# A four-mixer decoder layer on one core: key mixer, query and value mixers and latent attention rewritten, and the schedule made with other operation times

## The chip, the core and the metric

The kernel runs on one NeuronCore of a Trainium2 chip. Its engines work side by side, each through a queue of its own in order: TensorE (PE in the profile; its weight loads are PEld), VectorE (DVE), ScalarE (ACT), GpSimd (POOL) and SyncE (SP), which here only issues transfers. The metric is the device time of one execution in microseconds (us), the median of several runs.

## The reference

One layer on x of 512 positions and 1024 channels, float32:

```python
h = rms_norm(x, norm1_g)
proj = h @ w_in                       # columns shared by four mixers and the gates
o_a = gated_deltanet(...)             # 4 heads of 128; conv + silu, decay, delta rule
o_b = latent_attention(...)           # 4 heads, 128 plain + 64 rotary dimensions, qk-norm
o_c = spatial_gating(...)             # u * (W_s v + b), W_s lower triangular 128x128
o_d = forgetting_attention(...)       # softmax logits + cumulative log forget gate
projected = einsum("bsiw,iwd->bsid", [o_a, o_b, o_c, o_d], w_branch)
x = x + (sum(sigmoid(gates) * projected)) @ w_out
x = x + square(relu(rms_norm(x) @ w_ff1)) @ w_ff2
```

Inside gated_deltanet, k is normalised per head, `lower = strict(k_beta k^T * decay)` is formed per chunk, and `(I + lower)^-1` is applied to the values and to the decayed keys; q enters through `q k^T * decay`. In latent_attention a logit is the dot product of 128 plain and of 64 rotated dimensions.

## The kernel before, in words

All large products keep float32 accuracy through three matmuls: each operand is split into a high part hi (rounded by ScalarE, L85) and a low part lo (the difference, by VectorE, L86), and `mm3` (L163 to L166) adds hi.hi, hi.lo and lo.hi. Weights come in units of 128x1024: the transfer into `raw` (L116, three buffers, issued by SP), the split into whi and wlo (L85, L86, three buffers), and 24 matmuls of 512 columns. `wunit` (L155) hands out one unit; before that it calls `tick`, which moves every open generator in `gens` on to its next `yield`. All side work (the mixers, the attentions) is written as such generators, so a `yield` means: let one more unit of matmuls go first.

That order of the text is not the final one. The framework's scheduler puts the instructions of each engine in an order: by its own operation times it asks which instructions are ready, and takes of these the one that stands first in the text. The queues are then fixed, with semaphores where an engine must wait for another. Tiles of one tag share the number of buffers in `BUFS` (L35).

The order of the stages: normalisation of x and a first small product (to L415); four key heads, `conv(4 + h)` (L617: ScalarE's product, three VectorE multiply-adds L623, tanh L614, VectorE's product L615 into knT); four units for the spatial gate's u; four for its v; four query heads, four value heads, four for z (L837 to L847); then the gate and branch projections (`branch`, L916) with the scan, latent attention and forgetting attention beside them; the output projection; and the up and down projections with a Strassen-like scheme (L208 to L282).

What the change touches:
- `kmix` (L654), one generator per key head: transposes knT (L657), sums its squares on ScalarE (L660), copies it to kn (L662), loads the head's cumulative decay to all partitions (gb, L668), forms exp(min(gb - gcc, 0)) in UA (VectorE L673, ScalarE L675), times br (GpSimd L676), a masked copy dm (GpSimd L684), then UA = (k k^T) * eb (L686) and the scaled keys KG and KD (GpSimd L688, L689).
- `inverse` (L720): copies the 32x32 diagonal blocks of UA through DRAM (scr, L723) into UB (L725), inverts them in a recurrence of 31 steps on VectorE (L732, L733), and goes on to 128x128 with matmuls.
- `colsum` (L635) and `qmix` (L823): ScalarE's square of a query head into sq (L637), then eight matmuls with a column of ones (L640). `vmix` (L829): transposes a value head. `sgmix` (L796): the spatial gate, at its end the split into oC.
- `mla_rope` (L1105), `mla_tr` (L1115): transposes of q, k, kr and qo; q and k are copied out of PSUM by ScalarE (L1117, L1121), kr and qo by VectorE (L1125). Two heads share one tile qrT, 64 rows each.
- `mla_mm` (L1128): per head and query block one matmul of 128 rows (L1131), one of the head's 64 rows (L1132) and the mask (L1133), each float32 one as two instructions in the trace. `fox_mm` (L1199, matmul at L1200) is its counterpart in forgetting attention, with 128 rows alone.

Of the kernel before, what the change touches and what calls it, by code (L numbers as in the profile page):

```python
# [31 lines left out]
    0, 1536, 2048, 2504, 3016, 3528, 5064, 5068)  # L32
AHEAD, AHEAD_RAW = 2, 3
ROWS = (20, 12, 7, 3)
BUFS = dict(ab=4, A=4, K=4, Q=4, G=4, V=4, R=4, U=4, S=8, cv=4, tr=6)  # L35


@with_exitstack
def trunk(ctx, tc, x, positions, norm1_g, w_in, dn_conv_w, dn_a_log, dn_dt_bias, dn_out_norm_g,
# [18 lines left out]
    def tsl(t):  # L58
        return slice(t * P, (t + 1) * P)
# [21 lines left out]
    def mbank():  # L81
        return psm.tile([P, 512], F32, tag="m", name="m")
# [549 lines left out]
        A.activation(out=s_, in_=src, func=AF.Square)  # L632
        V.tensor_reduce(out=dst, in_=t3(s_), axis=AX.X, op=ALU.add)

    def colsum(src):  # L635
        s_ = W("sq")
        A.activation(out=s_, in_=src, func=AF.Square)  # L637
        pb = mbank()
        for t in range(NT):
            T.matmul(out=pb[:, t:t + 1], lhsT=s_[:, tsl(t)], rhs=one, start=True, stop=True)  # L640
        return pb[:, :NT]

    ssk = small([H, NT], "ssk")
    cm5p = small([16], "cm5p")
    ssq = small([H, NT], "ssq")
# [8 lines left out]
    def kmix(h, kT):  # L654
        yield
        KNT[h] = kT
        pk = tpose(cols(kT))  # L657
        sq = W("sq")
        for t in range(NT):
            A.activation(out=sq[:, tsl(t)], in_=pk[:, tsl(t)], func=AF.Square, accum_out=ssk[:, h, t:t + 1])  # L660
        kn = W("kn")
        A.activation(out=kn, in_=pk, func=AF.Copy)  # L662
        V.tensor_scalar(out=ssk[:, h, :], in0=ssk[:, h, :], scalar1=4 * EPS, scalar2=None, op0=ALU.add)
        rk2 = small([NT], "rk2", bufs=2)
        V.reciprocal(out=rk2, in_=ssk[:, h, :])
        yield
        gb = EGB[h] = W("egb", "Q")
        SY.dma_start(out=gb, in_=cumd[h].partition_broadcast(P))  # L668
        br = small([NT], "br", bufs=2)
        V.tensor_tensor(out=br, in0=rk2, in1=beta[:, :, h], op=ALU.mult)  # L670
        eb = UA[:, hsl[h], :]
        for t in range(NT):
            V.tensor_scalar(out=eb[:, t, :], in0=gb[:, tsl(t)], scalar1=gcc[:, t, h:h + 1], scalar2=0.0,  # L673
                            op0=ALU.subtract, op1=ALU.min)
        A.activation(out=eb, in_=eb, func=AF.Exp)  # L675
        G.tensor_tensor(out=eb, in0=eb, in1=last(br, P), op=ALU.mult)  # L676
        glv = t3(gb)[:, :, P - 1]
        V.tensor_tensor(out=ekd[:, h, :], in0=glv, in1=gcc[:, :, h], op=ALU.subtract)
        A.activation(out=ekd[:, h, :], in_=ekd[:, h, :], func=AF.Exp)
        V.scalar_tensor_tensor(out=ekd[:, h, :], in0=ekd[:, h, :], scalar=-1.0, in1=br, op0=ALU.mult, op1=ALU.mult)  # L680
        A.activation(out=egl[:, h, :], in_=glv, func=AF.Exp)
        A.activation(out=gb, in_=gb, func=AF.Exp)
        dm = DM[h] = W("dm", "A")
        G.tensor_tensor(out=t3(dm), in0=eb, in1=mid(maskI, NT), op=ALU.mult)  # L684
        yield
        V.tensor_tensor(out=eb, in0=t3(mm4(kT, kT)), in1=eb, op=ALU.mult)  # L686
        KG[h], KD[h] = W("kg", "G"), W("kd", "K")
        G.tensor_tensor(out=t3(KG[h]), in0=t3(kn), in1=last(eg[:, :, h], P), op=ALU.mult)  # L688
        G.tensor_tensor(out=t3(KD[h]), in0=t3(kn), in1=last(ekd[:, h, :], P), op=ALU.mult)  # L689

    flat = "p t f -> p (t f)"
    DS = [(D0[:, hsl[h], :].rearrange(flat), DT0[:, hsl[h], :].rearrange(flat)) for h in range(H)]
# [25 lines left out]
                                in1=py[r_, :8 * s].rearrange("p (m f) -> p m f", f=s), op=ALU.subtract)  # L718

    def inverse():  # L720
        for b in range(4):
            bs = slice(32 * b, 32 * b + 32)
            SY.dma_start(out=scr[:, b].rearrange("h j i -> j h i"), in_=UA[bs, :, bs])  # L723
        for q in range(2):
            SY.dma_start(out=UB[64 * q:64 * q + 64], in_=scr.rearrange("h b j i -> (h b) j i"))  # L725
        V.memset(UB.rearrange("p j i -> p (j i)")[:, 0:1024:33], -1.0)
# [69 lines left out]
    def sgmix():  # L796
        for t in range(NT):
            sumsq(rsg[:, t, :], vs[t])
        rsqrt(rsg, rsg, 16, 1.0 / P, EPS, shape=4)
        for t in range(NT):  # L800
            G.tensor_tensor(out=t3(vs[t]), in0=t3(vs[t]), in1=last(rsg[:, t, :], P), op=ALU.mult)
        yield
        V.tensor_tensor(out=t3(wsT), in0=t3(tpose(cols(ws))), in1=mid(maskI, 4), op=ALU.mult)
        yield
        yield
        for g in range(4):
            gs = tsl(g)
            pb = mbank()
            for t in range(NT):
                T.matmul(out=pb[:, tsl(t)], lhsT=vs[t][:, gs], rhs=wsT[:, gs], start=True, stop=True)  # L810
            s_ = W("oc_")
            V.scalar_tensor_tensor(out=t3(s_), in0=t3(pb), scalar=par(R_SG + g), in1=mid(bsb[:, gs], NT),
                                   op0=ALU.mult, op1=ALU.add)
            G.tensor_tensor(out=uT[g], in0=s_, in1=uT[g], op=ALU.mult)
            if g % 2 == 1:
                yield
        for g in range(4):
            oC[g] = WR("oc", "S")
            split(oC[g][0], oC[g][1], uT[g])
# [2 lines left out]

    def qmix(h, qT):  # L823
        yield
        V.tensor_copy(out=ssq[:, h, :], in_=colsum(qT))
        G.tensor_tensor(out=EGB[h], in0=EGB[h], in1=qT, op=ALU.mult)
        V.scalar_tensor_tensor(out=AT[h], in0=mm4(KNT[h], qT), scalar=-1.0, in1=AT[h], op0=ALU.mult, op1=ALU.mult)

    def vmix(h, vT):  # L829
        yield  # L830
        VT[h] = W("v", "V")
        V.tensor_tensor(out=t3(VT[h]), in0=t3(tpose(cols(vT))), in1=last(ssk[:, h, :], P), op=ALU.mult)
# [268 lines left out]
        rsqrt(rq_, rq_, 8, 1.0 / 192, EPS, post=192.0 ** -0.5, shape=2)  # L1101

    def mla_rope(c):
        kr, qo = W("kr"), W("qo")
        krv = kr.rearrange("p (t h f) -> p t h f", h=2, f=64)  # L1105
        V.tensor_tensor(out=krv, in0=krr.unsqueeze(2).broadcast_to([P, NT, 2, 64]),
                        in1=last(rkm[:, :, 2 * c:2 * c + 2], 64), op=ALU.mult)
        qov = qo.rearrange("p (t h f) -> p t h f", h=2, f=64)
        tmp = W("tmp")[:, :256].rearrange("p (t h f) -> p t h f", h=2, f=32)
        tb4 = [tabs[0][:, n].unsqueeze(2).broadcast_to([P, NT, 2, 32]) for n in range(4)]  # L1110
        rope(V, qov, qrv[c][:, :, :, 0:32], qrv[c][:, :, :, 32:64], tb4, tmp)
        return kr, qo

    def mla_tr(c, kr, qo):
        for hh in range(2):  # L1115
            qT = W("qT", "V")
            A.activation(out=qT, in_=tpose(hslice(qns[c], hh)), func=AF.Copy)  # L1117
            qTs.append(qT)
        for hh in range(2):
            kT = W("kT", "G")  # L1120
            A.activation(out=kT, in_=tpose(hslice(kns[c], hh)), func=AF.Copy, scale=gqk[:, 0:1])  # L1121
            kTs.append(kT)
        for src, dst in ((kr, krT), (qo, qrT)):
            r_ = W("krT", "R")
            V.tensor_copy(out=r_, in_=tpose(cols(src)))  # L1125
            dst.append(r_)

    def mla_mm(h, i, ps):  # L1128
        ro = slice(64 * (h % 2), 64 * (h % 2) + 64)
        w = (i + 1) * P  # L1130
        T.matmul(out=ps, lhsT=qTs[h][:, tsl(i)], rhs=kTs[h][:, :w], start=True, stop=False)  # L1131
        T.matmul(out=ps, lhsT=qrT[h // 2][ro, tsl(i)], rhs=krT[h // 2][ro, :w], start=False, stop=False)  # L1132
        T.matmul(out=ps[:, i * P:w], lhsT=identb, rhs=mbias, start=False, stop=True)  # L1133

    def mla_post(h, i, ps, pm, e_):
# [215 lines left out]
```

## Time and profile before

| | us |
|---|---|
| median of three runs | 1034.23 |
| lowest and highest | 1033.84, 1034.94 |
| the profiled execution | 1034.64 |
| its span, first to last instruction | 1032.9 |
| TensorE busy in it | 1010.1 |

The granted TensorE clock is 0.994 of full speed over the span. A busy TensorE in this profile is not one at its peak: the ends of matmuls are modelled and overlap the next start, so pitch is read from starts. A wait is listed with the instruction that waited, the one that released it, the total, the number and the longest. A busy time of a window counts all instructions that overlap it.

### The profile page before, as it was taken

What the parts mean: (1) busy time and instruction counts of PE and PEld (TensorE: products, weight loads), DVE (VectorE), ACT (ScalarE), POOL (GpSimd) and SP (SyncE); (2) the same over time, 40 slices, a digit from 0 to 9 for tenths busy, and PEclk for the clock granted to TensorE, in tenths of its full rate; (3) what the DMA queues carried; (4) which work ended last, traced back from release to release, by engine and by line L of the source; (5) the groups of instructions that cost most, each with busy time, mean ns of one, the idle gap of its engine ahead of it and who ended that gap; (6) DMA issues with size and microseconds to landing.
All of it is one profiled execution on the core that took longest, in us unless ns stands there. A gap on an engine that the chain in (4) does not pass through costs nothing.

```text
span 1032.9 us, 12908 instructions
## 1 busy us (share of the span) xinstructions
PE 1010.1 (98%) x4995; PEld 833.9 (81%) x4995; DVE 610.0 (59%) x992; ACT 422.8 (41%) x724; POOL 172.8 (17%) x210
## 2 busy tenths in 40 slices
PE   7989989999999989999999999999999999999998
PEld 6878877888888867778888888888888888888886
DVE  7784899623654754433365443447687598598541
ACT  6463334332433533434444333245453344256420
POOL 2553235100300420015154021100000000000000
PEclk9999989999999999999999999999999999999999
DMA  6334334212223232222422333337135125211421
GB/s 200 103 103 112 102 69 94 72 55 81 62 84 111 62 102 62 82 62 82 123 81 63 98 106 102 96 114 242 38 102 172 36 79 183 62 42 35 129 77 66
DMA packets 127621, 96.69 MB, mean 94 GB/s; under 512 B 15732, under 2 KB 112064, under 8 KB 127560
## 3 DMA queue, kind: packets, MB, share of 16 engines
q1 hardware_dynamic: 127480, 95.85, 31.6%
q8 instruction: 39, 0.64, 0.3%
q14 instruction: 22, 0.18, 0.1%
q10 hardware_dynamic: 80, 0.03, 0.0%
HBM read 92.96 MB, written 2.90 MB: 93 GB/s over the span
## 4 chain that ended last, share of the span: by engine, by line
PE 86%; DVE 8%; DMA 2%; issue 1%; ACT 1%; POOL 1%; SPq 0%; ACTq 0%; DVEq 0%; POOLq 0%
PE g L164 23%; PE g L166 23%; PE g L165 23%; PE m L164 2%; PE m L165 2%; PE m L166 2%; PE m L986 2%; DMA raw<-in_w_in_dram 2%; PE m L196 1%; DVE wlo L86 1%; PE m L205 1%; PE m L1132 1%; DVE cv L623 1%; PE m L976 1%; PE m L1131 1%
## 5 line engine op out<-in xcount | busy, mean ns | idle before, releaser
L86 DVE TENSOR_TENSOR wlo<-raw,whi 128x1024 fp32r<-128x1024 f32 (+2 forms) x136 | 175.4, 1290 | 229.0 <-ACT whi L85 219.6
L85 ACT ACTIVATE whi<-raw 128x1024 fp32r<-128x1024 f32 (+2 forms) x136 | 142.7, 1049 | 319.3 <-PE g L165 155.3
L164 PE MATMUL g<-h,whi 128*128 128x512 f32 x416 | 167.9, 404 | 0.0
L166 PE MATMUL g<-h,wlo 128*128 128x512 f32 x416 | 164.1, 394 | 0.0
L165 PE MATMUL g<-h,whi 128*128 128x512 f32 x416 | 163.5, 393 | 0.0
L164 PE MATMUL g<-xT,whi 128*128 128x512 f32 x256 | 99.7, 389 | 0.0
L166 PE MATMUL g<-xT,wlo 128*128 128x512 f32 x256 | 99.6, 389 | 0.0
L165 PE MATMUL g<-xT,whi 128*128 128x512 f32 x256 | 99.6, 389 | 0.0
L166 PEld LDWEIGHTS g<-h,wlo 128*128 128x128 f32 x416 | 78.9, 190 | 16.7
L164 PEld LDWEIGHTS g<-h,whi 128*128 128x128 f32 x416 | 78.9, 190 | 16.2 <-issue 0.5
L165 PEld LDWEIGHTS g<-h,whi 128*128 128x128 f32 x416 | 78.9, 190 | 16.0 <-issue 0.5
L939 POOL TENSOR_TENSOR mg<-mg,tg 128x512 f32<-128x512 f32 x24 | 35.6, 1487 | 194.2 <-DVE tg L935 193.9
L166 PEld LDWEIGHTS g<-xT,wlo 128*128 128x128 f32 x256 | 48.1, 188 | 10.0
L164 PEld LDWEIGHTS g<-xT,whi 128*128 128x128 f32 x256 | 48.1, 188 | 10.0
L165 PEld LDWEIGHTS g<-xT,whi 128*128 128x128 f32 x256 | 48.1, 188 | 9.9
L164 PE MATMUL g<-whi,h 128*128 128x512 f32 x128 | 50.8, 397 | 0.0
L166 PE MATMUL g<-whi,h 128*128 128x512 f32 x128 | 49.9, 390 | 0.0
L165 PE MATMUL g<-wlo,h 128*128 128x512 f32 x128 | 49.9, 389 | 0.0
L164 PE MATMUL m<-whi,ah 128*128 128x512 f32 x96 | 37.3, 389 | 0.0
L165 PE MATMUL m<-wlo,ah 128*128 128x512 f32 x96 | 37.3, 389 | 0.0
L166 PE MATMUL m<-whi,al 128*128 128x512 f32 x96 | 37.3, 389 | 0.0
L86 DVE TENSOR_TENSOR wlo<-T,whi 128x1024 fp32r<-128x1024 f32 x18 | 22.0, 1220 | 11.5 <-ACT whi L85 11.4
(404 smaller groups left out, 1988.7 us busy)
## 6 DMA issues: line engine op xcount, KB each, us to landing
raw<-in_w_in_dram SPq DMA_DIRECT2D x68, 512.0 KB
raw<-in_w_ff_dram SPq DMA_DIRECT2D x40, 512.0 KB
raw<-in_w_branch_dram SPq DMA_DIRECT2D x16, 512.0 KB
re<-in_w_ff_dram SPq DMA_DIRECT2D x6, 1024.0 KB
ro<-in_w_ff_dram SPq DMA_DIRECT2D x6, 1024.0 KB
raw<-in_w_out_dram SPq DMA_DIRECT2D x8, 512.0 KB
x<-in_x_dram SPq DMA_DIRECT2D x4, 512.0 KB
x<-in_x_dram SPq DMA_DIRECT2D x8, 256.0 KB
```

The costliest lines, as they stand in the source:

```text
L85: A.activation(out=hi, in_=src, func=AF.Copy)
L86: V.tensor_tensor(out=lo, in0=src, in1=hi.bitcast(F32), op=ALU.subtract)
L164: T.matmul(out=ps, lhsT=lh, rhs=rh, start=start, stop=False, skip_group_check=more)
L165: T.matmul(out=ps, lhsT=lh, rhs=rl, start=False, stop=False, skip_group_check=more)
L166: T.matmul(out=ps, lhsT=ll, rhs=rh, start=False, stop=stop, skip_group_check=more)
L196: T.transpose(out=pb[:, tsl(t)], in_=srcs[t], identity=ident)
L205: T.matmul(out=pb[:, tsl(t)], lhsT=lhsT[:, tsl(t)], rhs=rhs[:, tsl(t)], start=True, stop=True)
L623: V.scalar_tensor_tensor(out=y[:, 3 - k:], in0=ps[:, :n], scalar=par(R_CONV + 12 * k + blkno), in1=y[:, 3 - k:], op0=ALU.mult, op1=ALU.add)
L939: G.tensor_tensor(out=merged[m], in0=merged[m], in1=tgs[b], op=ALU.add)
L976: T.transpose(out=pb[:, tsl(t)], in_=pms[n][:, tsl(t)], identity=ident)
L986: T.matmul(out=pv[:, tsl(m)], lhsT=vblk(h, j), rhs=pts[n][:, o_ + j * P:o_ + (j + 1) * P], start=(j == 0), stop=(j == i))
L1131: T.matmul(out=ps, lhsT=qTs[h][:, tsl(i)], rhs=kTs[h][:, :w], start=True, stop=False)
```

## The change

The buffers of three tags grow, and the framework's descriptor scratch in on-chip memory shrinks from 16384 to 1024 bytes a partition. `kmix` forms exp(-relu(gcc - gb)) on ScalarE straight into dm, sends the diagonal blocks of UA head by head, and does the mask and the scaled keys later; `sgmix`, `qmix` and `vmix` get more yields; latent attention's rotary q is kept per head in a 128-row tile whose other half is zero, and ScalarE does all copies out of PSUM; the scheduler takes its operation times from its timeline simulator. The main lines:

```diff
-BUFS = dict(ab=4, A=4, K=4, Q=4, G=4, V=4, R=4, U=4, S=8, cv=4, tr=6)
+BUFS = dict(ab=4, A=4, K=4, Q=4, G=4, V=4, R=6, U=4, S=8, cv=8, tr=8)
@@ kmix
-        kn = W("kn")
-        A.activation(out=kn, in_=pk, func=AF.Copy)
+        KG[h] = W("kg", "G")
+        A.activation(out=KG[h], in_=pk, func=AF.Copy)
-        eb = UA[:, hsl[h], :]
-        for t in range(NT):
-            V.tensor_scalar(out=eb[:, t, :], in0=gb[:, tsl(t)], scalar1=gcc[:, t, h:h + 1], scalar2=0.0,
-                            op0=ALU.subtract, op1=ALU.min)
-        A.activation(out=eb, in_=eb, func=AF.Exp)
-        G.tensor_tensor(out=eb, in0=eb, in1=last(br, P), op=ALU.mult)
+        dm = DM[h] = W("dm", "A")
+        for t in range(NT):
+            A.activation(out=dm[:, tsl(t)], in_=gb[:, tsl(t)], func=AF.Relu, scale=-1.0, bias=gcc[:, t, h:h + 1])
+        A.activation(out=dm, in_=dm, func=AF.Exp, scale=-1.0)
+        G.tensor_tensor(out=t3(dm), in0=t3(dm), in1=last(br, P), op=ALU.mult)
-        dm = DM[h] = W("dm", "A")
-        G.tensor_tensor(out=t3(dm), in0=eb, in1=mid(maskI, NT), op=ALU.mult)
         yield
-        V.tensor_tensor(out=eb, in0=t3(mm4(kT, kT)), in1=eb, op=ALU.mult)
-        KG[h], KD[h] = W("kg", "G"), W("kd", "K")
-        G.tensor_tensor(out=t3(KG[h]), in0=t3(kn), in1=last(eg[:, :, h], P), op=ALU.mult)
-        G.tensor_tensor(out=t3(KD[h]), in0=t3(kn), in1=last(ekd[:, h, :], P), op=ALU.mult)
+        V.tensor_tensor(out=UA[:, hsl[h], :], in0=t3(mm4(kT, kT)), in1=t3(dm), op=ALU.mult)
+        for b in range(4):
+            bs = slice(32 * b, 32 * b + 32)
+            (A if h == H - 1 and b < 2 else SY).dma_start(out=scr[hsl[h], b].rearrange("h j i -> j h i"), in_=UA[bs, hsl[h], bs])
+        for _ in range(H - h):
+            yield
+        G.tensor_tensor(out=t3(dm), in0=t3(dm), in1=mid(maskI, NT), op=ALU.mult)
+        KD[h] = W("kd", "K")
+        G.tensor_tensor(out=t3(KD[h]), in0=t3(KG[h]), in1=last(ekd[:, h, :], P), op=ALU.mult)
+        G.tensor_tensor(out=t3(KG[h]), in0=t3(KG[h]), in1=last(eg[:, :, h], P), op=ALU.mult)
@@ inverse
-        for b in range(4):
-            bs = slice(32 * b, 32 * b + 32)
-            SY.dma_start(out=scr[:, b].rearrange("h j i -> j h i"), in_=UA[bs, :, bs])
@@ sgmix, before the split into oC
+        for _ in range(4):
+            yield
@@ qmix (colsum goes)
-        V.tensor_copy(out=ssq[:, h, :], in_=colsum(qT))
+        s_ = W("sq")
+        A.activation(out=s_, in_=qT, func=AF.Square)
+        yield
+        pb = mbank()
+        for t in range(NT):
+            T.matmul(out=pb[:, t:t + 1], lhsT=s_[:, tsl(t)], rhs=one, start=True, stop=True)
+        V.tensor_copy(out=ssq[:, h, :], in_=pb[:, :NT])
@@ vmix
         yield
+        yield
@@ mla_rope
+        for hh in range(2):
+            qrT.append(W("qrT", "R"))
+            G.memset(qrT[-1][64 - 64 * hh:128 - 64 * hh], 0.0)
@@ mla_tr
+        pb = tpose(cols(qo))
+        for hh in range(2):
+            r_ = qrT[2 * c + hh]
+            own = slice(64 * hh, 64 * hh + 64)
+            A.activation(out=r_[own], in_=pb[own], func=AF.Copy)
+        r_ = W("krT", "R")
+        A.activation(out=r_, in_=tpose(cols(kr)), func=AF.Copy)
+        krT.append(r_)
...
-        for src, dst in ((kr, krT), (qo, qrT)):
-            r_ = W("krT", "R")
-            V.tensor_copy(out=r_, in_=tpose(cols(src)))
-            dst.append(r_)
@@ mla_mm
-        T.matmul(out=ps, lhsT=qrT[h // 2][ro, tsl(i)], rhs=krT[h // 2][ro, :w], start=False, stop=False)
+        T.matmul(out=ps, lhsT=qrT[h][:, tsl(i)], rhs=krT[h // 2][:, :w], start=False, stop=False)
@@ kernel
-    nc = _bacc.Bacc("TRN2", target_bir_lowering=False, num_devices=1)
+    nc = _bacc.Bacc("TRN2", target_bir_lowering=False, num_devices=1, dynamic_dma_scratch_size=1024)
-    with _tile.TileContext(nc) as tc:
+    with _tile.TileContext(nc, schedule_with_timeline_sim=True) as tc:
```

## Rows read from the trace of the kernel before

**Rows 1.** Page, parts 1 and 5: busy us, share, instructions; a group: busy us, mean ns.

```profile
PE 1010.1 (98%) x4995; PEld 833.9 (81%) x4995; DVE 610.0 (59%) x992; ACT 422.8 (41%) x724; POOL 172.8 (17%) x210
...
L164 PE MATMUL g<-xT,whi 128*128 128x512 f32 x256 | 99.7, 389 | 0.0
```

**Rows 2.** Waits of PE: engine line <- releaser: total us, times, longest.

```profile
PE m L196 <- DVE knT L615: 4.0, 2, 2.7
...
PE m L640 <- ACT sq L637: 3.4, 1, 3.4
...
PE m L1132 <- DVE krT L1125: 2.3, 1, 2.3
...
PE m L196 <- DVE cv L615: 1.0, 1, 1.0
...
PE m L976 <- DVE Pm L967: 0.4, 1, 0.4
```

**Rows 3.** Windows: us, busy us of PE, PEld, DVE, ACT, POOL; PEclk; DMA.

```profile
46.00:80.00 34.00, 29.45 (x142) 23.95 (x142) 27.96 (x59) 21.44 (x66) 15.28 (x13) 0.95 0.32 94
...
75.90:79.20 3.30, 3.30 (x9) 2.56 (x8) 0.51 (x3) 3.29 (x12) 1.79 (x3) 0.51 0.03 5
...
80.00:100.00 20.00, 20.00 (x98) 16.83 (x97) 8.71 (x8) 4.64 (x6) 7.90 (x5) 1.00 0.44 104
...
104.00:148.00 44.00, 40.57 (x184) 34.03 (x184) 40.29 (x87) 14.56 (x20) 10.35 (x7) 0.92 0.31 85
...
134.60:140.80 6.20, 6.19 (x23) 5.61 (x24) 6.20 (x12) 0.63 (x1) 1.59 (x2) 0.50 0.25 75
...
740.00:760.00 20.00, 20.00 (x90) 16.57 (x89) 17.49 (x21) 12.24 (x18) 0.00 (x0) 1.00 0.13 34
```

**Rows 4.** Timeline, 65 to 76 us: start, duration, engine, line, operation.

```profile
65.17 1.04 POOL L676 TENSOR_TENSOR UA<-UA,br 128x512 f32<-128x512 f32 x1 [1.09 <-ACT UA L675]
...
65.22 1.00 DVE L680 SCALAR_TENSOR_TENSOR ekd<-ekd,br 128x4 f32<-128x4 f32 x1
...
75.15 0.66 PE L196 MATMUL m<-ident,knT 128*128 128x128 f32 x4 [2.71 <-DVE knT L615]
```

**Rows 5.** Groups by line, all shapes apart: busy us, mean ns.

```profile
L673 DVE TENSOR_SCALAR UA<-egb,gcc 128x128 f32<-128x128 f32 x16 | 5.7, 382 | 1.3 <-DMA egb<-cumd 1.3
...
L660 ACT ACTIVATE sq<-m 128x128 f32<-128x128 f32 x16 | 4.2, 276 | 1.4 <-PE m L196 1.4
```

**Rows 6.** Timeline of SP's queue, 92 to 99 us.

```profile
92.05 2.44 SPq L723 DMA_DIRECT2D scr<-UA  x4
...
98.32 1.16 SPq L725 DMA_DIRECT2D D<-scr  x2
```

**Rows 7.** Timeline, 361 to 371 us, latent attention's first scores.

```profile
361.50 1.28 ACT L1121 ACTIVATE kT<-m,gqk 128x512 f32<-128x512 f32 x2
...
367.64 1.06 ACT L85 ACTIVATE whi<-raw 128x1024 fp32r<-128x1024 f32 x1 [4.87 <-PE g L165]
...
367.79 1.22 DVE L86 TENSOR_TENSOR wlo<-raw,whi 128x1024 fp32r<-128x1024 f32 x1
...
368.92 1.28 DVE L1125 COPY krT<-m 128x512 f32<-128x512 f32 x2
...
370.26 0.48 PE L1132 MATMUL m<-krT 64*128 64x128 f32 x2 [2.26 <-DVE krT L1125]
```

**Rows 8.** Timeline of PE, latent attention's scores of 256 keys.

```profile
443.44 0.60 PE L1131 MATMUL m<-kT,qT 128*128 128x256 f32 x2
443.97 0.70 PE L1132 MATMUL m<-krT 64*128 64x256 f32 x2
444.60 0.23 PE L1133 MATMUL m<-mbias,identb 128*128 128x128 bf16 x1
```

**Rows 9.** Timeline of PE, forgetting attention's scores of 256 keys, twice.

```profile
560.58 1.03 PE L1200 MATMUL m<-kT,qT 128*128 128x256 f32 x4
561.26 0.58 PE L164 MATMUL g<-h,whi 128*128 128x512 f32 x1
```

More of the change, by code (lines that the diff above doesn't have):

```diff
@@ L633, in sumsq @@
         V.tensor_reduce(out=dst, in_=t3(s_), axis=AX.X, op=ALU.add)
[L635 to L638, printed above, removed]
-        for t in range(NT):
-            T.matmul(out=pb[:, t:t + 1], lhsT=s_[:, tsl(t)], rhs=one, start=True, stop=True)
-        return pb[:, :NT]
     ssk = small([H, NT], "ssk")
@@ L1122, in mla_tr @@
             kTs.append(kT)
-        for src, dst in ((kr, krT), (qo, qrT)):
-            r_ = W("krT", "R")
-            V.tensor_copy(out=r_, in_=tpose(cols(src)))
-            dst.append(r_)
     def mla_mm(h, i, ps):
-        ro = slice(64 * (h % 2), 64 * (h % 2) + 64)
         w = (i + 1) * P
         T.matmul(out=ps, lhsT=qTs[h][:, tsl(i)], rhs=kTs[h][:, :w], start=True, stop=False)
-        T.matmul(out=ps, lhsT=qrT[h // 2][ro, tsl(i)], rhs=krT[h // 2][ro, :w], start=False, stop=False)
+        T.matmul(out=ps, lhsT=qrT[h][:, tsl(i)], rhs=krT[h // 2][:, :w], start=False, stop=False)
         T.matmul(out=ps[:, i * P:w], lhsT=identb, rhs=mbias, start=False, stop=True)
```

## The prediction

> **What bounds the kernel now.** The page's first part comes first: TensorE is busy 98% of the span, VectorE 59%, ScalarE 41%, GpSimd 17% [rows 1]. A matmul's bar is longer than its pitch (0.389 us [rows 1] against 90 starts in 20 us, one per 0.22 us [rows 3]), so the share says only that TensorE almost always has work. A change off TensorE can therefore return only what TensorE waits, what it runs at the lower clock, and what a matmul loses between its neighbours. So the second view is TensorE's waits [rows 2]. Leaving out the start and the tail, five entries matter: 4.0 us on knT in two waits, 3.4 us on sq, 2.3 us on krT, 1.0 us on cv, 0.4 us on Pm. The third view is the windows [rows 3]. After two of these waits the granted clock stands at the lower level, 1.2 GHz: 3.30 us at 0.51 behind the 2.71 us wait for knT, and 6.19 busy us at 0.50 behind the 3.4 us wait for sq [rows 2 to 4]. Behind shorter waits no row shows it. In the down projection's windows (740 to 760 us) TensorE has no gap at all.
>
> The windows also name the cause. Between 46 and 80 us VectorE works 27.96 of 34 us, between 104 and 148 us 40.29 of 44 us; between 80 and 100 us it works 8.71 of 20 [rows 3]. TensorE's order is fixed when the program is made, so a consumer placed too early stops every matmul behind it.
>
> **Part 1, the key mixer.** The four decay subtractions per head leave VectorE: 16 instructions, 5.7 us [rows 5]. ScalarE takes 16 Relu instead; the nearest row, a 128x128 activation, is 0.276 us, so 4.4 us, on an engine with 21.44 of 34 us used [rows 3, 5]. Three GpSimd products per head (a product of that shape took 1.04 us [rows 4]) move one to four weight units later, to where VectorE works 8.71 of 20 us [rows 3]. This helps VectorE too: while a GpSimd product ran from 65.17 to 66.21 us, a VectorE operation on 128x4 elements took 1.00 us, in the same microsecond [rows 4]. VectorE's 28 us thus fall to about 22 of 34, and knT is no longer late. Gain: 4.0 us of waits, and 3.30 x 0.49 = 1.6 us of clock. I take all 5.6; the lower bound is nothing, if the order still asks for knT early.
>
> The Trainium skill (ScalarE: Activation LUTs, Rules for kernel authors) speaks against this edit: relu and min belong on VectorE, which it calls up to about three times as fast per element. In this trace the 128x128 form takes 0.382 us on VectorE and 0.276 us on ScalarE [rows 5], so the rule doesn't hold for these shapes here. By it the move would load ScalarE as in rival C.
>
> The copies of UA's diagonal blocks go out per head: 16 transfers instead of 4. Four issues took 2.44 us, 0.61 each [rows 6], so 14 on SP's queue are 8.5 us and two on ScalarE's 1.2 us. On SP each now waits for its head's product, and the weight loads behind it wait too; three raw weight buffers, each one unit of 24 matmuls x 0.22 = 5.3 us, cover that. In exchange the read-back into UB, issued at 98.32 us, 6.3 us behind the first copy [rows 6], can start earlier, and so can the 31-step recurrence that fills VectorE from 104 to 148 us. No charge, a few us of slack.
>
> **Part 2, the query and value mixers.** qmix now puts one unit (5.3 us) between ScalarE's square and the eight column-sum matmuls; vmix waits one unit more before its transposes; the split of oC moves four units back. The two waits are 3.4 and 1.0 us, both below one unit, so both go; the clock gives back 6.19 x 0.50 = 3.1 us. Together 7.5 us. The delayed work is covered by the units of the v and z projections. Longer-lived tiles are what the added buffers (R, cv, tr) are for; taken alone they cost no time, and what they need is what the smaller descriptor scratch frees.
>
> **Part 3, latent attention.** The copies of kr and qo out of PSUM leave VectorE. Before, krT came at 368.92 us, because VectorE's queue held a weight split ahead of it that waited for a ScalarE split, which itself had waited 4.87 us for TensorE; the scores' second matmul waited 2.26 us [rows 7]. On ScalarE, ahead of the four q and k copies, they are done several us before the scores. Gain 2.3 us. ScalarE now makes seven copies of about 0.64 us (two took 1.28 us [rows 7]) per pair of heads for six sets of transposes, and four PSUM banks must turn over: up to 1 us of new waiting per pair. I charge 1.0 for both. What is queued behind is one ScalarE weight split, which has a unit in hand. The four zero fills are GpSimd work in a stretch where that engine is idle.
>
> The second score matmul goes from 64 rows to 128. Its pair of instructions for 256 keys holds TensorE 0.63 us (443.97 to 444.60), the full-height pair before it 0.53 us [rows 8]; in forgetting attention four full-height instructions of that size are followed by the next stream's first matmul 0.68 us after their start, and that one runs 0.19 us over its usual 0.39 [rows 1], so 0.87 us for two pairs, 0.435 each [rows 9]. There are 16 such pairs, one for each head and query block. Lower bound: only 0.63 becomes 0.53, 16 x 0.10 = 1.6 us. Upper bound: both pairs become 0.435, 16 x (0.095 + 0.195) = 4.6 us. I take 4.0, near the upper end, since after the change every neighbour is full height as in rows 9.
>
> The Trainium skill (TensorEngine Tiling (Array Packing), Performance Considerations) speaks against the padding: a contraction of 64 or less is the case for row tiling, up to twice as fast. The 64-row pair here is the slower one [rows 8], since the kernel never runs two such tiles side by side. By that rule the padding would cost what rival D says.
>
> **Part 4, the order.** The scheduler gets other operation times, so which ready instruction comes next on an engine may change anywhere. No row of before shows that order. One bound: it removes nothing beyond the above and adds nothing. The other: a new wait like the present ones. I charge 2.5 us, five waits like the 0.4 to 0.5 us one on Pm [rows 2], and keep the large case as rival B.
>
> **Sum.** The profiled execution took 1034.64 us (span 1032.9 us), 0.4 us over the median. 1034.6 - 5.6 - 7.5 - 2.3 - 4.0 + 1.0 + 2.5 = 1018.7; against the median **1018.5 us**.
>
> **Rivals.**
> A: the waits stay. If TensorE's queue still asks for knT and for the column sums before VectorE can deliver, part 1 and part 2 give nothing: 1034.6 - 2.3 - 4.0 + 1.0 = 1029. For it: 27.96 and 40.29 us of VectorE work are lowered, not gone. Against: one unit exceeds both waits of part 2.
> B, slower: the new order puts consumers too early where TensorE has no gap now, above all in the up and down projections, where VectorE works 17.49 of 20 us [rows 3]. One wait like that on sq costs 3.4 us and 3.1 us of clock, 6.5 us. The gains are 16 us, so it decides from the third such wait: 1018.5 + 19.5 = 1038. Against it: today's order has none in those windows, with the same matmuls and weights.
> C: ScalarE becomes the bound of the key stage. It has 34 - 21.4 = 12.6 us free [rows 3], which 16 Relu fill from 0.79 us each. At 1.00 us, the longest short operation shown [rows 4], they need 16.0 us: the stage grows by 3.4 us and part 1's 5.6 us are lost, 1018.5 + 9.0 = 1027.5. Against it: the 0.276 us of [rows 5].
> D: padding doubles the 64-row matmuls. Sixteen pairs, taken at the 0.63 us of 256 keys [rows 8], add 10.1 us in place of the 4.0 gained: 1018.5 + 14.1 = 1032.6, within 0.2%.
>
> **Chances.** Forecast 0.51, A 0.18, B 0.22, C 0.04, D and other ways of ending level 0.05. Faster by over 0.2% (2 us, about what a measurement here can tell from no change) 0.73, within 0.05, slower 0.22. The forecast's own range is 1013 (upper end of part 3, no new waits, a us of slack from the recurrence) to 1024. To leave out at most two in ten it must reach A and most of B: 1012 to 1038.
>
> **What would show it.** Waits of TensorE on knT, sq and krT gone from the list; granted clock 1.00 between 46 and 150 us; VectorE near 22 us of the first 34-us stretch; the score pairs of 256 keys at 0.44 us each; the recurrence starting before 104 us. Wrong if TensorE shows new waits above 2 us behind 200 us, or if the waits stay where they are on other tiles.

## The result, and the profile after

The changed kernel takes **1020.2 us** (median; 1018.7 to 1022.0 in four runs), the kernel before 1034.3 us in the same series: a ratio of 0.9864, 95% interval 0.9846 to 0.9882. The forecast was 1018.5 us. The profiled execution took 1018.67 us, with a span of 1017.0 us. The number was met, inside a stated range of 1012 to 1038 us that is wide enough to hold no change as well; the runs below show that it was not met for the reasons given.

The page after, parts 1 and 5 (columns as in [rows 1]):

```profile
PE 1001.8 (99%) x4995; PEld 833.3 (82%) x4995; DVE 603.4 (59%) x972; ACT 435.3 (43%) x748; POOL 171.1 (17%) x214
...
L164 PE MATMUL g<-xT,whi 128*128 128x512 f32 x256 | 99.5, 390 | 0.0
```

TensorE's waits after (columns as in [rows 2]). The first two lines are the start of the program:

```profile
PE m L380 <- DVE dg L376: 3.4, 1, 3.4
PE m L357 <- POOL identb L608: 3.1, 1, 3.1
PE m L824 <- ACT sq L820: 2.6, 2, 1.6
PE g L164 <- ACT abh L85: 0.8, 1, 0.8
PE m L695 <- DVE D L743: 0.7, 1, 0.7
```

The waits on knT, cv, krT and Pm of [rows 2] are gone. The one on sq is not: 3.4 us in one wait have become 2.6 us in two. Behind 180 us the list is empty.

Windows after (columns as in [rows 3]):

```profile
46.00:80.00 34.00, 34.00 (x176) 28.39 (x175) 22.43 (x44) 23.72 (x72) 11.67 (x10) 1.00 0.34 98
...
80.00:100.00 20.00, 20.00 (x94) 16.69 (x93) 9.36 (x19) 10.42 (x21) 10.96 (x8) 1.00 0.56 139
...
100.00:150.00 50.00, 47.26 (x244) 39.66 (x242) 48.87 (x90) 19.61 (x28) 17.33 (x11) 1.00 0.34 92
...
150.00:156.00 6.00, 6.00 (x27) 5.07 (x28) 6.00 (x11) 2.58 (x4) 3.05 (x3) 0.72 0.75 128
164.00:170.00 6.00, 5.99 (x73) 4.39 (x72) 5.96 (x10) 1.78 (x4) 0.67 (x2) 0.72 0.32 84
```

Read these in two halves. In the key stage (46 to 80 us) TensorE has no gap left and VectorE works 22.43 us, as forecast. In the mixers' stretch VectorE is full, 48.87 of 50 us, and behind 150 us there are two stretches of 6 us at a mean granted clock of 0.72, each worth 6 x 0.28 = 1.7 us.

**A table by stage.** TensorE starts 3696 weight matmuls of 128x512 (lines 164 to 166) in every one of these kernels. When the Nth of them starts, the same amount of weight work is done, whatever the order around it. Counted in the timeline, the 241st starts when the key mixers are ending, the 1057th ahead of the attention stages, the 1901st behind them. What a kernel gains on the kernel before between two of these is its gain in that stage. In the kernel before they start at 106.31, 353.68 and 618.04 us; in the changed kernel at 99.67, 346.23 and 602.03 us. So the change gains 6.6 us up to the end of the key stage, 0.8 us in the mixers' stage, 8.6 us in the attention stages and 0.25 us behind them: 16.3 us up to the last weight matmul. (The spans differ by 15.9 us. The medians differ by 14.1 us, for the profiled execution was the fastest of the four.) The forecast had 5.6, 7.5 and 5.3 us for the three stages, and 2.5 us lost to the order.

### The profile page after: what moved, and what is told of

Its sections match the earlier page's. It is cut to its first block, busy times and chain, and to the rows that moved or that the text cites. A ratio compares the mean times of both kernels' runs of the same rounds, so it can differ in the third digit from the quotient of the medians.

```text
span 1017.0 us, 12919 instructions
## 1 busy us (share of the span) xinstructions
PE 1001.8 (99%) x4995; PEld 833.3 (82%) x4995; DVE 603.4 (59%) x972; ACT 435.3 (43%) x748; POOL 171.1 (17%) x214
## 4 chain that ended last, share of the span: by engine, by line
PE 86%; DVE 6%; DMA 3%; ACT 2%; issue 1%; SPq 1%; POOL 0%; ACTq 0%; DVEq 0%
PE g L166 23%; PE g L164 23%; PE g L165 23%; PE m L165 2%; PE m L166 2%; PE m L164 2%; PE m L987 2%; PE m L196 2%; DVE D L725 1%; DVE wlo L86 1%; DVE xw L724 1%; PE m L1138 1%; PE m L977 1%; PE m L1207 1%; PE m L1139 1%
## 6 DMA issues: line engine op xcount, KB each, us to landing
re<-in_w_ff_dram SPq DMA_DIRECT2D x6, 1024.0 KB, 5.2
ro<-in_w_ff_dram SPq DMA_DIRECT2D x6, 1024.0 KB, 5.0
```

## The experiments

The changed kernel is parts 1 (key mixer), 2 (query and value mixers), 3 (latent attention) and 4 (the order). The runs undo one part, or do some of them alone. Each ratio is against runs of the kernel before on the same chip. "Place" is the number of column-sum copies (ssq) that stand on VectorE's queue ahead of the four block products into D0; its use comes further down; in the kernel before it is 3.

The three stage columns come from one profiled execution of each kernel. How far they can be trusted shows in the changed kernel and e3_rope64, which run the same instructions in the same order on every engine up to 200 us, on TensorE up to 358 us: their columns differ by 0.8 us (key) and 1.1 us (mixers). The attention column repeats to 0.1 us: 8.5 to 8.6 in every kernel with all of part 3 under the new order, 4.3 in both without it.

| kernel | parts | median us | ratio (95%) | key | mixers | attention | place |
|---|---|---|---|---|---|---|---|
| changed kernel | 1 2 3 4 | 1020.2 | 0.9864 (0.9846 to 0.9882) | 6.6 | 0.8 | 8.6 | 3 |
| e1_default_order | 1 2 3 | 1025.7 | 0.9904 (0.9888 to 0.9919) | 3.6 | 0.0 | 5.3 | 2 |
| e2_order_alone | 4 | 1020.3 | 0.9852 (0.9836 to 0.9867) | 6.0 | 4.0 | 4.3 | 4 |
| e3_rope64 | 1 2 4, 3 without padding | 1024.2 | 0.9889 (0.9872 to 0.9906) | 5.9 | -0.3 | 3.8 | 3 |
| e4_mixers_back | 1 3 4 | 1024.0 | 0.9893 (0.9869 to 0.9917) | 6.5 | -4.7 | 8.6 | 2 |
| r5_order_attn | 3 4 | **1014.3** | 0.9814 (0.9798 to 0.9829) | 6.6 | 5.3 | 8.6 | 4 |
| r6_order_key | 1 4 | 1029.5 | 0.9958 (0.9942 to 0.9974) | 6.1 | -4.6 | 4.3 | 2 |
| r7_order_attn_relief | 3 4, VectorE relieved | 1016.5 | 0.9832 (0.9813 to 0.9852) | 6.2 | 4.1 | 8.6 | |
| r8_order_attn_mixers | 2 3 4 | 1017.8 | 0.9841 (0.9822 to 0.9861) | 6.1 | 0.6 | 8.6 | 3 |
| h1_e4_hold | 1 3 4, products held | 1020.7 | 0.9857 (0.9843 to 0.9872) | 6.3 | -1.3 | 8.6 | 4 |
| h2_after_hold | 1 2 3 4, products held | 1016.6 | 0.9823 (0.9807 to 0.9839) | 6.6 | 4.1 | 8.5 | 4 |
| x1_key_copies_late | 1 3 4, copies as before | 1025.0 | 0.9902 (0.9887 to 0.9917) | 6.3 | -5.5 | 8.6 | 2 |
| x3_relu_only | 3 4, Relu alone of 1 | 1019.4 | 0.9847 (0.9831 to 0.9863) | 6.7 | -1.7 | 8.6 | 4 |

### Is it the order or the edits?

Two theories at first. S: VectorE is full in the mixers' stretch whatever the order, so what part 2 should bring is lost there. O: the new order put the column sums too early.

**e1_default_order**, the changed kernel with the old operation times:

```diff
-    with _tile.TileContext(nc, schedule_with_timeline_sim=True) as tc:
+    with _tile.TileContext(nc) as tc:
```

> The changed kernel, scheduled with the framework's own operation times again (the whole of part 4 undone, parts 1 to 3 kept). Theory S: in the stretch of the query mixer VectorE is full whatever the order (48.87 of 50 us between 100 and 150 us), so the column sums still wait for the SiLU products there and the clock still falls: 1018 to 1024 us, with over 2 us of waits on sq, cv or D before 200 us. Theory O: it is the new order that puts the column sums and the block products too early; with the old operation times the waits on sq are gone and the 6.6 us that part 2 owes come in: about 1014 us.

Measured: 1025.7 us, outside both numbers. The edits alone, in the old order, are worth 9.9 us of 1035.5, not the 18.4 us forecast for them. The mixers' stage gains nothing here either, and new waits stand in the list: 2.4 us on D, 2.1 us on Pm, 1.4 us still on knT. A window of this kernel (columns as in [rows 3]) and its wait on knT (as in [rows 2]):

```profile
46.00:80.00 34.00, 32.24 (x167) 26.74 (x165) 25.55 (x43) 25.87 (x77) 11.91 (x11) 1.00 0.35 98
```

```profile
PE m L196 <- DVE knT L615: 1.4, 1, 1.4
```

The consumers stand where they stood in the kernel before (the transposes of knT behind 148, 168, 192 and 216 weight matmuls), VectorE works 25.55 us in place of 27.96, and the wait on knT falls from 4.0 to 1.4 us: with a lighter VectorE it is shorter, not gone.

**e2_order_alone**, the kernel before with that one line added.

> The kernel before with nothing but the simulated operation times in the scheduler. If the order alone brings none of the gain, 1032 to 1037 us, and the waits on knT, sq and krT stand in the list at 1 us or more each. If the order is what took away the waits on knT and krT (and the padding and the yields did little), 1026 us or less.

Measured: **1020.3 us**. The order alone is worth as much as the whole change (0.9852 against 0.9864). The waits on knT are gone with VectorE no lighter. A window of this kernel (columns as in [rows 3]):

```profile
46.00:80.00 34.00, 34.00 (x176) 28.39 (x175) 29.55 (x65) 22.92 (x70) 13.32 (x11) 1.00 0.37 109
```

And its timeline, VectorE's products that make knT and TensorE's transposes of knT, for the last two heads:

```profile
65.71 0.69 DVE L615 SCALAR_TENSOR_TENSOR knT<-th,cv 128x512 f32<-128x512 f32 x1
...
70.20 0.60 PE L196 MATMUL m<-ident,knT 128*128 128x128 f32 x4
...
75.63 0.90 DVE L615 SCALAR_TENSOR_TENSOR knT<-th,cv 128x512 f32<-128x512 f32 x1 [0.81 <-ACT th L614]
...
78.14 0.60 PE L196 MATMUL m<-ident,knT 128*128 128x128 f32 x4
```

VectorE works 29.55 of 34 us, more than the 27.96 of [rows 3], and the product that makes the last knT starts later than before (75.63 against 74.42 us in the kernel before). But TensorE doesn't wait, for its queue asks later: the four transposes of knT stand behind 182, 183, 219 and 248 weight matmuls (the narrower ones of the gates counted too), where the kernel before has them behind 148, 168, 192 and 216. The wait on krT falls from 2.3 to 0.2 us in the same way. So the load alone doesn't make the wait. It comes from a consumer that stands ahead of the time at which its producer is done: a later place takes the wait away whole (e2), a lighter producer in part (e1).

**e3_rope64** goes back to 64 rows and one packed tile per pair of heads:

```diff
-        T.matmul(out=ps, lhsT=qrT[h][:, tsl(i)], rhs=krT[h // 2][:, :w], start=False, stop=False)
+        ro = slice(64 * (h % 2), 64 * (h % 2) + 64)
+        T.matmul(out=ps, lhsT=qrT[h // 2][ro, tsl(i)], rhs=krT[h // 2][ro, :w], start=False, stop=False)
```

> The changed kernel with the second score matmul back on 64 rows and one packed tile per pair of heads; all else kept. Summed by own pitch, the score matmuls of after hold TensorE 4.8 us less than before's (3.1 in the second matmul itself, 1.7 in its neighbours): if that is the price of the padding, 1025.0 us. If the neighbours' 1.7 us come from the order of the work and not from the row count, 1023.3 us. If the extra gain of the attention stage is the order's alone, 1021 us or less.

Measured: 1024.2 us, and in the attention stages 3.8 us in place of 8.6: the padding is worth 4.8 us there. r5 against e2 (8.6 against 4.3) gives 4.3 us, with part 3's copies in it. The whole times say less: the ratios of e3 and of the changed kernel are 2.6 us apart and their intervals overlap. The timeline of TensorE in the changed kernel, scores of 256 keys, to be held against [rows 8]:

```profile
452.83 0.60 PE L1138 MATMUL m<-kT,qT 128*128 128x256 f32 x2
453.26 0.59 PE L1139 MATMUL m<-krT,qrT 128*128 128x256 f32 x2
453.69 0.22 PE L1140 MATMUL m<-mbias,identb 128*128 128x128 bf16 x1
```

The pairs start 0.43 us apart (453.26 and 453.69), where the 64-row pair held TensorE 0.63 us and its neighbour 0.53 us.

**e4_mixers_back** takes part 2's units out of qmix, vmix (one) and sgmix (four), and leaves the added buffers; qmix's:

```diff
         A.activation(out=s_, in_=qT, func=AF.Square)
-        yield
         pb = mbank()
```

> The changed kernel with the added units of qmix, vmix and sgmix taken out again (part 2 undone, parts 1, 3 and 4 kept). Theory S: the delay of one unit was used up by a later VectorE, so it is worth little by itself: 1020 to 1023 us. Rival: the delay is worth the forecast 7.5 us and something else in the changed kernel costs 6.6 us there: 1026 to 1028 us, with the wait on sq at 3 us or more and a longer stretch at the lower clock.

Measured: 1024.0 us, between the two. In the mixers' stage it loses 4.7 us on the kernel before, while e2, which has neither part 1 nor part 2, gains 4.0. So theory S falls too: VectorE is as full in e2 (48.87 of 50 us between 100 and 150 us, the same as after). A new theory: under the new order part 1 costs in that stage, part 2 buys some of it back, and parts 3 and 4 alone are the better kernel.

### What each part is worth under the new order

**r5_order_attn** is the kernel before with parts 3 and 4 (R=6, the smaller descriptor scratch, the zero fills, the copies on ScalarE, the full-height matmul, the scheduler's line).

> The kernel before with the new order and part 3 (padding, copies on ScalarE, more R buffers, smaller descriptor scratch); parts 1 and 2 left out. If order and padding add up and parts 1 and 2 are not needed once the order is new: 1020.3 - 4.9 = 1015.4 us (4.9 us is the padding's worth between e3_rope64 and the changed kernel in the attention stage), faster than both kernels. If parts 1 and 2 carry a share that the order alone can't hold, 1019 us or more.

Measured: **1014.3 us**, 0.9814 (0.9798 to 0.9829). It beats the kernel before and the changed kernel, whose interval lies wholly above it.

**r6_order_key** is the kernel before with parts 1 and 4; of part 1, beside the Relu and the tile dm in UA's place:

```diff
+        for b in range(4):
+            bs = slice(32 * b, 32 * b + 32)
+            (A if h == H - 1 and b < 2 else SY).dma_start(out=scr[hsl[h], b].rearrange("h j i -> j h i"), in_=UA[bs, hsl[h], bs])
+        for _ in range(H - h):
+            yield
```

> The kernel before with the new order and part 1 alone (Relu on ScalarE, deferred products, copies of UA per head). By stage, e2_order_alone gains 5.0 us in the query mixer's stretch and e4_mixers_back, which has part 1 beside the order, loses 4.6 us there. If it is part 1 that costs this, 1025 to 1030 us, with the loss between 100 and 200 us. If the difference came from the order that the scheduler happened to find, 1019 to 1022 us.

Measured: 1029.5 us. In the key stage it gains what e2 gains (6.1 against 6.0 us): part 1 adds nothing there. In the mixers' stage it loses 4.6 us where e2 gains 4.0. Part 1 costs 8.6 us, all of it in a stage that it hardly touches. A window of this kernel and the same one of e2 (columns as in [rows 3]):

```profile
150.00:180.00 30.00, 24.20 (x173) 20.15 (x174) 26.82 (x40) 9.70 (x15) 17.18 (x12) 0.83 0.46 96
```

```profile
150.00:180.00 30.00, 27.05 (x226) 22.05 (x227) 29.84 (x44) 11.68 (x18) 16.31 (x12) 1.00 0.48 106
```

TensorE has 5.8 us of gaps here where e2 has 2.95, and its clock of 0.83 is worth another 30 x 0.17 = 5.1 us: together 8.0 of the 8.6 us. That is no accident of one execution: the mean granted clock is 0.994 to 0.995 in all four executions of this kernel and 0.998 to 1.000 in e2's.

**r8_order_attn_mixers** is r5 with part 2.

> The kernel of r5_order_attn with part 2 added (all of the change but part 1). If part 2's units help under the new order as they do beside part 1 (5.5 us between e4_mixers_back and the changed kernel in that stretch), they take most of the 3.6 us of gaps left there: about 1012 us. If the order already did what the units are for, 1015 to 1016 us. If it lands at 1020 us like the full change, part 1 is not what costs in that stretch.

Measured: 1017.8 us. Part 2 costs here (0.6 us in the mixers' stage against 5.3), though beside part 1 it brings 5.5 (0.8 against -4.7). The profiled execution is the slowest of its four; by the medians, on one chip, part 2 costs 3.4 us. Its largest loss stands at one place. The timeline of VectorE and of TensorE, and a window behind it:

```profile
166.80 1.27 DVE L743 TENSOR_TENSOR D<-comp,dmask 128x512 f32<-128x512 f32 x1 [2.33 <-DMA comp<-scrD]
...
168.18 0.60 PE L692 MATMUL m<-D,UA 32*32 32x32 f32 x8 [3.11 <-issue]
```

```profile
168.00:172.00 4.00, 3.34 (x26) 3.17 (x27) 4.00 (x5) 0.37 (x1) 2.92 (x3) 0.50 0.04 11
```

TensorE stands 3.11 us ahead of the first block of the inverse with no releaser shown, and then runs at the lower level, 1.2 GHz. The first of the block products, which the inverse's matmuls read, ends at 168.07 us, 0.11 us before TensorE goes on, and had itself waited 2.33 us for its transfer. That makes the product the likely releaser; the profile doesn't name it.

**r7_order_attn_relief** is r5 with VectorE relieved behind 100 us; the largest of its three edits:

```diff
-            V.tensor_tensor(out=D0[:, hsl[h], :].rearrange("p t (b f) -> p t b f", f=32), in1=dm4, op=ALU.mult,
-                            in0=comp[:, hsl[h], :].unsqueeze(2).broadcast_to([P, NT, 4, 32]))
+                    A.activation(out=D0[:, h2, 32 * b:32 * b + 32], in_=comp[:, h2, :], func=AF.Copy,
+                                 scale=dmask[:, 32 * b:32 * b + 1])
```

> The kernel of r5_order_attn with VectorE relieved between 100 and 170 us: the four block products into D0 (4.6 us) become eight scaled copies on ScalarE, the copy of XB (1.1 us) goes to ScalarE, and the four sums of squares of sgmix are accumulated by ScalarE's squares. If the waits of that stretch come from VectorE's load, the 3 to 4 us of gaps that e2_order_alone has between 140 and 170 us go: 1011 to 1013 us. If the order alone decides, 1015.4 us with the gaps merely elsewhere.

Measured: 1016.5 us, no faster than r5 although VectorE works 120.27 us between 46 and 200 us in place of 126.97. The windows, first of r5, then of this kernel:

```profile
140.00:170.00 30.00, 26.72 (x159) 22.57 (x160) 29.93 (x43) 10.56 (x17) 17.94 (x15) 1.00 0.42 88
```

```profile
140.00:170.00 30.00, 27.71 (x216) 22.50 (x216) 26.72 (x39) 16.52 (x29) 18.51 (x15) 0.94 0.42 89
```

Taking 6.7 us off the engine that is full shortened TensorE's gaps there only from 3.3 to 2.3 us, and a clock of 0.94, worth 1.8 us, came in their place.

### What of part 1 costs?

The timeline of VectorE names a suspect. In r5_order_attn, the copies of the column sums and the products into D0:

```profile
136.26 0.15 DVE L825 COPY ssq<-m 128x4 f32<-128x4 f32 x1
...
146.89 0.15 DVE L825 COPY ssq<-m 128x4 f32<-128x4 f32 x1
...
159.18 0.15 DVE L825 COPY ssq<-m 128x4 f32<-128x4 f32 x1
...
161.29 0.15 DVE L825 COPY ssq<-m 128x4 f32<-128x4 f32 x1
...
165.41 2.48 DVE L751 TENSOR_TENSOR D<-comp,dmask 128x512 f32<-128x512 f32 x4
```

And in e4_mixers_back, which has part 1 besides:

```profile
139.80 0.15 DVE L822 COPY ssq<-m 128x4 f32<-128x4 f32 x1
...
150.55 0.15 DVE L822 COPY ssq<-m 128x4 f32<-128x4 f32 x1
...
160.23 4.35 DVE L743 TENSOR_TENSOR D<-comp,dmask 128x512 f32<-128x512 f32 x4 [1.48 <-DMA comp<-scrD]
...
166.31 0.15 DVE L822 COPY ssq<-m 128x4 f32<-128x4 f32 x1
...
167.57 0.15 DVE L822 COPY ssq<-m 128x4 f32<-128x4 f32 x1
```

There the products have come ahead of two column sums. VectorE waits 1.48 us for their transfer, works on them 4.35 us, and the weight splits, convolution taps and copies behind them wait 5.8 us.

**h1_e4_hold** keeps e4 and holds the products back by data; it also starts them three units later, with seven `yield`s in place of four:

```diff
+        if h == H - 1:
+            V.scalar_tensor_tensor(out=dmk, in0=ssq[:, h, 0:1].broadcast_to([P, P]), scalar=0.0, in1=dmask,
+                                   op0=ALU.mult, op1=ALU.add)
...
-        for _ in range(4):
+        for _ in range(7):
             yield
...
-            dm4 = dmask.rearrange("p (b f) -> p b f", f=32).unsqueeze(1).broadcast_to([P, NT, 4, 32])
+            dm4 = dmk.rearrange("p (b f) -> p b f", f=32).unsqueeze(1).broadcast_to([P, NT, 4, 32])
```

> The kernel of e4_mixers_back (order, parts 1 and 3: 1024.0 us) with one thing more: the block products into D0 and DT0 read a copy of their mask that is written after the fourth column sum, so that VectorE can't take them ahead of the query mixers; one small VectorE operation more. In e4_mixers_back the four products (4.35 us) stand on VectorE's queue after the second of the four copies of column sums, in r5_order_attn (1014.3 us) after the fourth. If this place is what costs, 1014 to 1018 us. If it is a symptom and VectorE's load or something else of part 1 costs, 1022 us or more, the inverse being later besides.

Measured: 1020.7 us, between the two. Place and later start together are worth 3.4 us of the mixers' stage (-1.3 against -4.7); they were not tried apart. The other 6.6 us to r5 are something else: two waits on sq take 3.4 us (2.3 in r5), and TensorE runs 6.8 us at 1.2 GHz (156.96 to 163.79 us), worth 3.4 us, which r5 doesn't. The rest wasn't followed.

**h2_after_hold** is the same hold in the changed kernel, with the start four units later (eight in place of four).

> The changed kernel with the same hold. Its products stand after the third copy of a column sum, and its mixer stretch is 4.1 us behind that of e2_order_alone. If the place costs, 1015 to 1018 us; if not, 1020 to 1023 us.

Measured: 1016.6 us, ratio 0.9823 (0.9807 to 0.9839) against the changed kernel's 0.9864 (0.9846 to 0.9882): a gain clear of the noise, 3.3 us of it in the mixers' stage. The stretch from 160 to 180 us, where the changed kernel lost its second 6 us at a clock of 0.72, has neither gap nor lower clock now:

```profile
160.00:180.00 20.00, 20.00 (x97) 16.56 (x96) 18.46 (x27) 5.83 (x9) 12.83 (x11) 1.00 0.32 90
```

**x1_key_copies_late** is r5 with part 1, but the copies of UA's blocks stay together:

```diff
     def inverse():
+        for b in range(4):
+            bs = slice(32 * b, 32 * b + 32)
+            SY.dma_start(out=scr[:, b].rearrange("h j i -> j h i"), in_=UA[bs, :, bs])
```

> The kernel of r5_order_attn with part 1, but the copies of UA's blocks stay four, together, at the head of the inverse as before. If the copies per head, which let the recurrence start earlier, are what makes part 1 lose 9.7 us, 1014 to 1016 us. If the loss lies in the rest of part 1 (in this kernel the block products stand after the second copy of a column sum again), 1023 to 1025 us.

Measured: 1025.0 us, with -5.5 us in the mixers' stage where r5 has 5.3. The copies per head are not what costs.

**x3_relu_only** is r5 with the Relu alone:

```diff
-            V.tensor_scalar(out=eb[:, t, :], in0=gb[:, tsl(t)], scalar1=gcc[:, t, h:h + 1], scalar2=0.0,
-                            op0=ALU.subtract, op1=ALU.min)
-        A.activation(out=eb, in_=eb, func=AF.Exp)
+            A.activation(out=eb[:, t, :], in_=gb[:, tsl(t)], func=AF.Relu, scale=-1.0, bias=gcc[:, t, h:h + 1])
+        A.activation(out=eb, in_=eb, func=AF.Exp, scale=-1.0)
```

> The kernel of r5_order_attn with the 16 decay subtractions as Relu on ScalarE and nothing else of part 1. The block products stay behind the fourth copy of a column sum. If the place decides, 1013 to 1016 us, and VectorE's 29.9 us between 46 and 80 us fall by some 5 us without bringing time, since TensorE has no gap there. If the Relu is what makes part 1 lose, 1020 us or more.

Measured: 1019.4 us, between the two numbers, and by a road that neither theory had. The timeline of VectorE and of TensorE, and then the start of the recurrence in r5:

```profile
94.95 0.69 DVE L685 TENSOR_TENSOR UA<-m,UA 128x512 f32<-128x512 f32 x1 [2.25 <-POOL dm L683]
...
106.35 0.09 DVE L725 MEMSET D<- 128x32 f32 x1 [9.58 <-DMA D<-scr]
...
106.94 1.22 DVE L86 TENSOR_TENSOR wlo<-raw,whi 128x1024 fp32r<-128x1024 f32 x1
108.07 0.15 DVE L732 TENSOR_REDUCE D<-xw 128x1 f32<-128x3 f32 x1
...
108.21 0.50 PE L165 MATMUL g<-wlo,h 128*128 128x512 f32 x1 [2.76 <-DVE wlo L86]
```

```profile
89.23 0.69 DVE L686 TENSOR_TENSOR UA<-m,UA 128x512 f32<-128x512 f32 x1 [2.25 <-POOL dm L684]
...
98.25 0.09 DVE L726 MEMSET D<- 128x32 f32 x1 [7.14 <-DMA D<-scr]
```

The order has the start of the recurrence ahead of a weight split. In r5 VectorE stands at the same point, for 7.14 us, and TensorE doesn't wait. With the Relu the last head's UA came 5.7 us later, the read-back landed later, VectorE stood 9.58 us, and TensorE waited 2.76 us for the split behind it. It is the same kind of fault at another place: an operation that waits for a transfer stands in front of one that TensorE needs.

The Relu has a price on ScalarE that the forecast left out. In the trace a table load stands where ScalarE goes from one kind of function to another, as from gelu to exp; one of x3:

```profile
77.77 1.28 ACT L674 ACT_TABLE_LOAD   x1
```

r5 has five of them; x3 and every kernel with part 1 under the new order have seven.

What of part 1 moves the products forward is not settled. Not the copies (x1: place 2 without them), not the Relu alone (x3: place 4). What remains are the deferred products and the tiles that changed with them, alone or together with the Relu; these were not tried apart.

## Why the prediction was right in its number and wrong in its reasons

**"The windows also name the cause"**: this is the step that failed first. VectorE's 27.96 of 34 us were taken for the reason of the late knT. e2_order_alone has 29.55 of 34 us and no wait. The sentence beside it, that a consumer placed too early stops everything behind it, names what the order alone mended; the lighter VectorE helps in the old order only in part (4.0 to 1.4 us in e1).

**Part 1**, forecast 5.6 us. The three signs came: no wait on knT, clock 1.00, VectorE at 22.43 us. The first two come with the order alone as well and couldn't tell it from the edit. The order alone brings 6.0 us in that stage, and part 1 with it 6.1. In the old order e1 gains 3.6 us there, with 1.4 us of knT left. "No charge" held for the copies (x1), but part 1 as a whole costs 8.6 us (r6 against e2), in a stage that the argument left out: it looked for room between 80 and 100 us, and not at VectorE's queue behind 140 us. The Relu was undersized too. The group in the changed kernel (columns as in [rows 5]):

```profile
L665 ACT ACTIVATE dm<-egb,gcc 128x128 f32<-128x128 f32 x16 | 5.3, 433 | 0.0
```

It keeps ScalarE busy 5.3 us, where 4.4 were charged, and VectorE's operation took 5.7 [rows 5]; one bar is 433 ns long against 382. The prediction had set the Trainium skill's rule aside here (ScalarE: Activation LUTs, Rules for kernel authors: relu and min belong on VectorE, up to about three times as fast in bf16). The factor is given for bf16, and the tiles here are float32. For this shape neither engine is faster to speak of: by the bar VectorE is, by the busy time ScalarE.

**Part 2**, forecast 7.5 us: 0.8 us in its stage. "Both are below one unit, so both go" took VectorE's queue as it was. In the changed kernel the SiLU product that the square needs is itself late, so two waits of 1.60 and 0.95 us came in the place of 3.4, with 0.7 us on D, and 3.4 us of lower clock. These sum to 6.7 us, as much as is missing. The recurrence did start earlier, at 98.8 us in place of 104, as forecast, but the order alone starts it at 99.4; its last reduction began at 147.00 us, against 147.52 before, on a VectorE that works 48.87 of 50 us. As an edit by itself part 2 costs 3.4 us under the new order (medians of r8 and r5; 4.7 us in the mixers' stage of the profiled executions) and brings 5.5 beside part 1 (changed kernel against e4, by stage).

**Part 3**, forecast 5.3 us. In the old order the sum was met, by luck in part: e1 gains 5.3 us in the attention stages, with 2.1 us of waits on Pm where 0.4 us stood before. Under the new order those stages gain 8.6. The padding was 4.3 to 4.8 us, at the upper bound given (4.6) and not at the 4.0 taken. The charge of 1.0 for ScalarE's copies didn't come: no wait on them is in the list. The krT wait went by the order alone as well. The Trainium skill's rule (TensorEngine Tiling (Array Packing), Performance Considerations: row tiling for a contraction of 64 or less) would have left the 64 rows. e3 shows the 128 rows faster here, where two 64-row tiles never run side by side; such a pair was not tried.

**Part 4**, charged with 2.5 us: wrong in sign and the largest error of all. Alone it gains 15.2 us (1035.5 to 1020.3). The bounds were "nothing" and "a loss"; that the present order could be bad was not among them, though the waits on knT and krT in [rows 2] were just that (4.0 and 2.3 us before, none and 0.2 us in e2).

**The rivals.** A's waits stayed only in part. B, the slower one, had the right mechanism, a consumer placed too early, at the wrong stage: behind 180 us TensorE has no wait, and the loss lies between 120 and 170 us. C and D fell: ScalarE worked 23.72 of 34 us in the key stage, and the padded pairs take 0.43 us.

**Why the sum came out.** By stage the forecast missed by +1.0 us (key), -6.7 (mixers), +3.3 (attention) and +2.75 (no loss to the order, and 0.25 us at the end): these cancel to 0.35 us in the profiled execution; the median is 1.7 us above the forecast. That the sum came out is luck. By part nothing fits: 13.1 us were credited to parts 1 and 2, the order alone brings 10.0 of the first two stages without them, and under the new order both together cost about 5 us (0.9814 for r5, 0.9864 for the changed kernel).

## What to carry to other kernels

A wait on a busy engine is first a question of where its consumer stands: count what stands ahead of the consumer on the waiting engine's queue before you lighten the producer, and try a different order by itself before you edit anything. When an order is made anew, edits that were planned for the old one have to be tried one by one under the new: here part 1 costs 8.6 us, and part 2 is a loss without part 1 and a gain beside it. Look on each in-order queue for an operation that waits for a transfer and stands ahead of work that the bounding engine needs; a data dependency that holds it back, with a start three or four units later, was worth 3.3 and 3.4 us of the mixers' stage here.

## What the runs showed beside

The length of a wait doesn't tell whether the clock falls. The prediction had it fall behind the long waits only [rows 2 to 4]. In the changed kernel it fell to the lower level behind a wait of 0.95 us; in e2_order_alone TensorE waited 2.26 us, and the clock stayed at 1.00. Both waits end in column sums and eight 128x128 matmuls. First the changed kernel, its timeline and a window behind the wait, then the same of e2:

```profile
149.50 1.05 PE L824 MATMUL m<-one,sq 128*128 128x1 f32 x8 [0.95 <-ACT sq L820]
```

```profile
152.00:154.00 2.00, 2.00 (x6) 1.60 (x5) 2.00 (x4) 1.52 (x2) 0.00 (x0) 0.50 0.60 61
```

```profile
156.43 1.05 PE L640 MATMUL m<-one,sq 128*128 128x1 f32 x8 [2.26 <-ACT sq L637]
```

```profile
150.00:158.00 8.00, 5.48 (x34) 4.65 (x35) 8.00 (x10) 3.85 (x6) 5.05 (x3) 1.00 0.10 37
```

Two executions of the same instructions differ as much. The changed kernel and e3_rope64 are the same up to here; both wait 1.6 us on the first sq, and only e3 falls, for 6.8 us. First the changed kernel, then e3:

```profile
131.30 1.05 PE L824 MATMUL m<-one,sq 128*128 128x1 f32 x8 [1.60 <-ACT sq L820]
```

```profile
132.20:139.00 6.80, 6.80 (x37) 5.81 (x37) 6.80 (x11) 1.84 (x3) 2.73 (x2) 1.00 0.16 40
```

```profile
131.63 1.38 PE L824 MATMUL m<-one,sq 128*128 128x1 f32 x8 [1.55 <-ACT sq L820]
```

```profile
132.20:139.00 6.80, 6.80 (x24) 5.83 (x24) 6.80 (x10) 2.17 (x4) 2.57 (x3) 0.50 0.15 40
```

So the program and the length of the wait don't fix whether the clock falls here, and a clock term of 1.7 or 3.4 us in one execution says little about the kernel; the mean clock of several executions says more. Why the one execution pays it and the other doesn't was not settled.
